# A hybrid decoder layer: the low parts of the input projection's weight tiles made by another engine

## The chip, the cores and the metric

The kernel runs on one core of a Trainium2 chip. The metric is the device time of one execution in microseconds; the median of three runs is compared. The engines are called as in the profile: PE is TensorE (matmul), PEld its weight loads, DVE is VectorE, ACT is ScalarE, POOL is GpSimd, SP is SyncE, which issues the transfers.

## The reference

One layer with a token mixer and a feed-forward part, for a prompt of 1024 positions and 8 x 4 sample positions. The mixer's three groups of heads read one normalised input through one combined input projection:

```python
hn = rms_norm(x, norm_mix_pre[l])
proj = jnp.einsum('bld,de->ble', h, w_in)            # ONE projection for all groups
conv_in, rest = proj[..., :CONV_DIM], proj[..., CONV_DIM:]
conv_out, new_conv = causal_dwconv(conv_in, conv_state, conv_w, conv_b)
conv_out = jax.nn.silu(conv_out)
...                                                   # gated DeltaNet, mLSTM, Mamba-2 SSD, in chunks
mix = jnp.concatenate([o_gdn, h_ml, y_ssd], axis=-1).astype(h.dtype)
out = jnp.einsum('ble,ed->bld', mix, w_out)
```

After it come a residual and a gated feed-forward part with a causal convolution. All inputs and outputs are fp32.

## The kernel before

A product of fp32 matrices is made of three passes in a reduced fp32 format. Each operand is cut into a high part (a cast) and a low part (the operand less its high part), and high x high, high x low and low x high are summed in PSUM (`dense`, lines 275 to 287). The input projection's weights are cut on the chip, tile by tile: `load_w` (lines 263 to 273) takes a tile of 128 x 1024 elements from HBM by a transfer from SP's queue (line 270, three buffers `w`), casts it on ScalarE (line 271, two buffers `wh`), and makes the low part by a subtraction (line 272, two buffers `wl`), on the engine whose operation is given as `tt`; where none is given that is POOL (`gtt`).

The projection has 32 tiles of 128 columns. Two are handled in `begin`, together with the normalisation, and a third is loaded there too (line 642, POOL). The other 29 come from `tile_w` (line 402), called by `gate`, `conv_tile` and `plain_tile`, in the order of the list FILL: the three tiles of each of eight units (four DeltaNet heads, two SSD groups, two mLSTM pairs), and eight gate tiles. Each tile is multiplied with the input in three groups of 352 columns; each group's result stands in one of two PSUM banks (`acc`) until DVE takes it out with a product (`scaled`, line 308). After that a convolved tile has an ACT instruction and three DVE instructions per group (line 473), a tanh on ACT and one more DVE instruction (line 482).

While TensorE works through these tiles, the recurrences of the heads run between them: the DeltaNet's inverse (lines 786 to 871, with line 792 among them), its scan (lines 996 to 1050: 1016 and 1031 on DVE), the SSD batches (lines 1176 to 1238: POOL's lines 1190, 1198 and 1205, DVE's 1189 and 1211), the mLSTM steps. In the first stretch the small rows of gates are made (lines 649 to 737: 703, 712, 720). The order of the work on TensorE is written out by hand, by a planner (`Weave`) that interleaves generators by rank and by times in the table WAIT; the projection has rank 9, the recurrences have ranks 0 to 5. The order on the other engines is made by the tile framework's scheduler from priorities: what has a rank below 8 gets a higher priority than the projection's instructions, its loads included, and otherwise the place in the program counts. Each engine and SP's queue then work through their own list in order. An instruction that has to wait holds what stands behind it.

Of the kernel before, what the change touches and what calls it, by code (L numbers as in the profile page):

```python
# [23 lines left out]
KD = D // P  # L24
# [29 lines left out]
TILE_ORDER = [(s, i) for _, _, ts in UNITS for s, i, _ in ts] + GATES  # L54
# [143 lines left out]
def kernel(ctx: ExitStack, tc: tile.TileContext, I, O):  # L198
# [24 lines left out]
    vtt = nc.vector.tensor_tensor  # L223
# [39 lines left out]
    def load_w(src, kk, w=None, parts=None, cuts=1, tt=gtt):  # L263

        if w is None:
            w = wp.tile([P, kk, P], F32, name="w", bufs=3)
        wh, wl = parts or [wp.tile([P, kk, P], F32R, name=f"w{x}") for x in "hl"]
        for c in range(cuts):
            ks = slice(kk * c // cuts, kk * (c + 1) // cuts)
            dma(out=w[:, ks], in_=src[:, ks])  # L270
            nc.scalar.copy(out=wh[:, ks], in_=w[:, ks])  # L271
            tt(out=wl[:, ks], in0=w[:, ks], in1=wh[:, ks].bitcast(F32), op=ALU.subtract)  # L272
        return wh, wl
# [99 lines left out]
    with ExitStack() as ph:  # L373
# [28 lines left out]
        def tile_w(s, i):  # L402
            if (s, i) in early:
                return early.pop((s, i))
            return load_w(I["w_in"][TILE_ORDER.index((s, i))], KD)

        gated = {}

        def gate(s, i, m):

            w = tile_w(s, i)
            room = cvp.tile([P, 1083], F32, name="pre") if s != "mo" else None
            x = room if s == "gg" else mix[m]
            for g in range(NG):
                a, b = g * G, (g + 1) * G
                ps = yield from dense(accp, w, hn_operand, KD, g)
                scaled(x[:, a:b], ps, g, 0, G)
                if s == "mo":
                    act(out=x[:, a:b], in_=x[:, a:b], func=AF.Tanh, scale=0.5)
                    continue  # L420
                th = room[:, groups[(g + 1) % NG]]
                act(out=th, in_=x[:, a:b], func=AF.Tanh, scale=0.5)

                n = b
                if s == "gg":
                    n = min(max(512 * min(max(done["outs"] - 2 * i, 0), 2), a), b)
                    gated[i] = b
                    if n < b:
                        stt(out=mix[m][:, n:b], in0=th[:, n - a:], scalar=1.0, in1=x[:, n:b], op0=ALU.add, op1=ALU.mult)
                if n > a:  # L430
                    stt(out=x[:, a:n], in0=th[:, :n - a], scalar=1.0, in1=x[:, a:n], op0=ALU.add, op1=ALU.mult)
                    if s == "gg":
                        vtt(out=mix[m][:, a:n], in0=mix[m][:, a:n], in1=x[:, a:n], op=ALU.mult)
# [23 lines left out]
        def conv_tile(s, i, t, y):  # L457
            begun = early_pre.pop((s, i), None)
            pre = conv_in(t) if begun is None else begun
            if begun is None:  # L460
                w = tile_w(s, i)
            blk = samples_of(pre)
            for g in range(NG):
                if begun is None:
                    ps = yield from dense(accp, w, hn_operand, KD, g)
                    conv_scaled(pre, ps, g)
                else:
                    yield lambda: rows_ln
                a, b = g * G, (g + 1) * G if g < 2 else 1080
                act(out=y[:, a:b], in_=pre[:, a + 3:b + 3], func=AF.Identity, bias=cw2[:, 72 + t:73 + t],  # L470
                    scale=cw2[:, 4 * t + 3:4 * t + 4])
                for j in (2, 1, 0):
                    stt(out=y[:, a:b], in0=pre[:, a + j:b + j], scalar=cw2[:, 4 * t + j:4 * t + j + 1], in1=y[:, a:b],
                        op0=ALU.mult, op1=ALU.add)
                if g == 2:
                    gcopy(out=conv_o[:, t, 0:3], in_=pre[:, 1024:1027])
                    gcopy(out=conv_o[:, t, 3:27].rearrange("p (b s) -> p b s", s=3), in_=blk[:, :, 4:7])

                th = act(out=pre[:, a:b], in_=y[:, a:b], func=AF.Tanh)
                if begun is not None:  # L480
                    in_order(th, rows_ln[0])
                stt(out=y[:, a:b], in0=pre[:, a:b], scalar=1.0, in1=y[:, a:b], op0=ALU.add, op1=ALU.mult)

        def plain_tile(s, i, y):
            w = tile_w(s, i)
            for g in range(NG):
                ps = yield from dense(accp, w, hn_operand, KD, g)
                if g < 2:
                    scaled(y[:, g * G:(g + 1) * G], ps, g, 0, G)
                else:  # L490
                    scaled(y[:, 2 * G:SEQ], ps, g, 0, 320)
                    scaled(samp(y), ps, g, 320, 352)
# [1727 lines left out]
```

## Time and profile before

| what | value |
|---|---|
| median of 3 runs | 1541.13 us (1540.32 to 1542.04) |
| the profiled execution's own time | 1540.03 us |
| its span, first to last instruction | 1538.2 us |
| PE busy | 1455.7 us (95%) |
| DVE busy | 1012.1 us (66%) |
| ACT busy | 604.9 us (39%) |
| POOL busy | 610.8 us (40%) |
| line 272 on POOL, tiles `wl`, whole kernel | 42 instructions, 105.2 us |

Busy times are of one profiled execution. An engine's line gives its busy time, its share of the span and its number of instructions. A group's line gives the line of the kernel, engine, operation, output and inputs, shape and count, then its busy time, the mean of one in ns, and the idle time just before its members with what ended it. A timeline's row gives the start and the duration in us, and in brackets the idle time in front of it and what ended that; rows of equal instructions in a row are merged ("x5"), and their duration is then that of all. The ends of matmuls are modelled.

### The profile page before, as it was taken

How to read it: one execution, taken by the hardware profiler on the slowest of the kernel's cores; microseconds unless marked ns; L12 is line 12 of the kernel's file. 1: busy time of each engine (PE TensorE's matmuls, PEld its weight loads, DVE VectorE, ACT ScalarE, POOL GpSimd, SP SyncE). 2: the span in 40 equal slices, each digit the busy share in tenths (PEclk: the TensorE clock that was granted, in tenths of full speed). 3: DMA queues.
4: the chain of work that ended last, by engine and by line, in shares of the span. 5: the costliest groups of instructions: out<-in, count | busy, mean ns of one | idle time of the engine just before them, and what ended most of it. 6: DMA issues, size and time to landing. Idle time of an engine off the chain costs nothing. (4 is left out here: it accounts for less than half of the span.)

```text
span 1538.2 us, 27512 instructions
## 1 busy us (share of the span) xinstructions
PE 1455.7 (95%) x10756; PEld 1410.1 (92%) x10756; DVE 1012.1 (66%) x2013; ACT 604.9 (39%) x1316; POOL 610.8 (40%) x672
## 2 busy tenths in 40 slices
PE   8888999989989989999999999999999999999997
PEld 8787998888989989889889999999999999999996
DVE  6889878697375457723679777766666685334447
ACT  7644544532432333423676433333333344202222
POOL 6234433341343464366641543444344341212234
PEclk9989999999999999999999999999999999999999
DMA  7111010100112032312640222122222136312304
GB/s 225 30 50 31 23 44 27 36 22 28 44 48 69 32 106 85 124 55 91 215 152 34 92 83 73 61 70 84 71 84 83 71 124 219 126 42 98 112 29 156
DMA packets 60362, 124.92 MB, mean 81 GB/s; under 512 B 15544, under 2 KB 21560, under 8 KB 59720
## 3 DMA queue, kind: packets, MB, share of 16 engines
q1 hardware_dynamic: 60232, 123.16, 24.3%
q8 instruction: 85, 1.39, 0.4%
q14 instruction: 45, 0.37, 0.1%
HBM read 97.40 MB, written 25.21 MB: 80 GB/s over the span
## 5 line engine op out<-in xcount | busy, mean ns | idle before, releaser
L208 PE MATMUL acc<-h,wh 128*128 128x264 f32 (+1 forms) x3008 | 672.1, 314 | 17.9 <-DVE pre L308 12.6
L208 PEld LDWEIGHTS acc<-h,wh 128*128 128x128 f32 x3008 | 491.8, 191 | 24.7 <-DVE pre L308 8.9
L208 PE MATMUL acc<-h,wl 128*128 128x264 f32 (+1 forms) x1512 | 462.0, 306 | 0.5 <-POOL wl L619 0.5
L208 PEld LDWEIGHTS acc<-h,wl 128*128 128x128 f32 x1512 | 287.7, 190 | 1.7 <-POOL wl L619 1.6
L208 PE MATMUL acc<-hidl,wh 128*128 128x264 f32 x576 | 163.7, 284 | 0.5 <-DVE hidl L2040 0.5
L208 PE MATMUL acc<-hidh,wh 128*128 128x264 f32 x576 | 163.9, 285 | 0.0
L208 PE MATMUL acc<-hidh,wl 128*128 128x264 f32 x576 | 163.5, 284 | 0.0
L1881 POOL TENSOR_TENSOR wl<-ws,wh 128x512 fp32r<-128x512 f32 x60 | 89.3, 1495 | 159.7 <-ACT wh L1880 155.1
L2063 DVE TENSOR_TENSOR fa<-fa,acc 128x264 f32<-128x264 f32 x160 | 68.3, 428 | 125.4 <-PE acc L208 124.7
L272 POOL TENSOR_TENSOR wl<-w,wh 128x1024 fp32r<-128x1024 f32 x42 | 105.2, 2505 | 68.3 <-ACT wh L271 65.5
L208 PE MATMUL acc<-n,wh 128*128 128x264 f32 x672 | 126.1, 284 | 0.0
L1881 POOL TENSOR_TENSOR wl<-w,wh 128x512 fp32r<-128x512 f32 x40 | 65.3, 1634 | 115.4 <-ACT wh L1880 115.4
L208 PEld LDWEIGHTS acc<-hidl,wh 128*128 128x128 f32 x576 | 108.6, 189 | 0.8 <-DVE hidl L2040 0.8
L208 PEld LDWEIGHTS acc<-hidh,wl 128*128 128x128 f32 x576 | 108.6, 189 | 0.0
L208 PEld LDWEIGHTS acc<-hidh,wh 128*128 128x128 f32 x576 | 108.5, 188 | 0.0
L2054 POOL TENSOR_TENSOR wl<-w,wh 128x1024 fp32r<-128x1024 f32 (+1 forms) x22 | 47.6, 2163 | 148.3 <-ACT wh L2053 145.3
L208 PEld LDWEIGHTS acc<-n,wh 128*128 128x128 f32 x672 | 103.9, 188 | 0.3 <-ACT sq L217 0.3
L208 PE MATMUL acc<-n,wl 128*128 128x264 f32 x336 | 96.1, 286 | 2.8 <-POOL wl L1881 2.8
L208 PE MATMUL acc<-r,wh 128*128 128x264 f32 x480 | 90.9, 286 | 2.8 <-DVE rs L1857 2.7
L208 PEld LDWEIGHTS acc<-r,wh 128*128 128x128 f32 x480 | 74.1, 188 | 4.9 <-DVE rs L1857 4.7
L1813 DVE SCALAR_TENSOR_TENSOR fy<-fpre,vec,fy 128x1072 f32<-128x1072 f32 x44 | 73.7, 1700 | 1.3 <-ACT fy L217 0.8
L2053 ACT CAST wh<-w 128x1024 fp32r<-128x1024 f32 (+1 forms) x22 | 20.5, 933 | 132.3 <-PE acc L208 127.7
(539 smaller groups left out, 3033.1 us busy)
## 6 DMA issues: line engine op xcount, KB each, us to landing
w<-in_w_in_dram SPq DMA_DIRECT2D x30, 512.0 KB
w<-in_w_up_dram SPq DMA_DIRECT2D x60, 256.0 KB
hid_dram<-hid SPq DMA_DIRECT2D x22, 528.0 KB
hidl<-hid_dram SPq DMA_DIRECT2D x21, 528.0 KB
w<-in_w_dn_dram SPq DMA_DIRECT2D x17, 512.0 KB
w<-in_w_out_dram SPq DMA_DIRECT2D x16, 512.0 KB
E<-rows_dram SPq DMA_DIRECT2D x24, 256.0 KB
n<-in_w_up_dram SPq DMA_DIRECT2D x20, 256.0 KB
```

Source lines behind the costliest of these rows:

```text
L208: return nc.tensor.matmul(out, **kw)
L272: tt(out=wl[:, ks], in0=w[:, ks], in1=wh[:, ks].bitcast(F32), op=ALU.subtract)
L1813: stt(out=y[:, :LF], in0=pre[:, j:j + LF], scalar=col(V_FW + 3 * f + j), in1=y[:, :LF], op0=ALU.mult, op1=ALU.add)
L1881: tt(out=wl, in0=x, in1=wh.bitcast(F32), op=ALU.subtract)
L2053: nc.scalar.copy(out=wh, in_=w)
L2054: gtt(out=wl, in0=w, in1=wh.bitcast(F32), op=ALU.subtract)
L2063: vtt(out=fa[:, q, m, :], in0=fa[:, q, m, :], in1=ps[:, :Q], op=ALU.add)
```

## The change

The subtraction of line 272 is issued to DVE (`vtt`) instead of POOL for the tiles that `tile_w` loads, 29 in number. The tile loaded at line 642, the two of `begin` (line 619) and all other users of `load_w` stay as they were.

```diff
         def tile_w(s, i):
             if (s, i) in early:
                 return early.pop((s, i))
-            return load_w(I["w_in"][TILE_ORDER.index((s, i))], KD)
+            return load_w(I["w_in"][TILE_ORDER.index((s, i))], KD, tt=vtt)
```

## Rows read from the trace of the kernel before

**Rows 1.** The page, busy time, share of the span and instructions of each engine.

```profile
PE 1455.7 (95%) x10756; PEld 1410.1 (92%) x10756; DVE 1012.1 (66%) x2013; ACT 604.9 (39%) x1316; POOL 610.8 (40%) x672
```

**Rows 2.** Stretches: length, busy PE, PEld, DVE, ACT, POOL; PE clock, DMA share, GB/s.

```profile
60.00:140.00 80.00, 64.05 (x357) 61.24 (x358) 72.48 (x166) 37.82 (x94) 30.07 (x48) 0.87 0.15 39
60.00:640.00 580.00, 533.37 (x3531) 511.51 (x3532) 416.17 (x1032) 232.72 (x661) 228.83 (x319) 0.97 0.17 49
```

**Rows 3.** Waits of PE, 45 to 640 us: total, times, longest.

```profile
PE acc L208 <- DVE pre L308: 12.6, 5, 4.3
```

**Rows 4.** Groups of POOL, 46 to 630 us.

```profile
L272 POOL TENSOR_TENSOR wl<-w,wh 128x1024 fp32r<-128x1024 f32 x29 | 71.8, 2476 | 44.4 <-ACT wh L271 41.6 <-PE po L208 2.4
```

**Rows 5.** Timelines of POOL and DVE about 106 us, DVE at 99.81.

```profile
106.02 2.40 POOL L272 TENSOR_TENSOR wl<-w,wh 128x1024 fp32r<-128x1024 f32 x1 [5.13 <-ACT wh L271]
...
106.37 2.43 DVE L482 SCALAR_TENSOR_TENSOR kq<-pre,kq 128x352 f32<-128x352 f32 x1 [0.73 <-ACT pre L217]
...
99.81 0.52 DVE L482 SCALAR_TENSOR_TENSOR kq<-pre,kq 128x352 f32<-128x352 f32 x1
```

**Rows 6.** Timeline of DVE beside the first and the last of the 29.

```profile
46.79 3.44 DVE L473 SCALAR_TENSOR_TENSOR kq<-li,cw,kq 128x352 f32<-128x352 f32 x2
...
622.62 2.88 DVE L1066 TENSOR_TENSOR gsq<-hml,gss 128x512 f32<-128x512 f32 x1 [1.75 <-POOL gss L1065]
```

**Rows 7.** Timeline of DVE, two subtractions of SBUF operands after 640 us.

```profile
650.57 1.25 DVE L1583 TENSOR_TENSOR h<-mix,h 128x1056 fp32r<-128x1056 f32 x1
...
738.18 1.59 DVE L272 TENSOR_TENSOR h<-w,h 128x1024 fp32r<-128x1024 f32 x1 [2.75 <-ACT h L271]
```

**Rows 8.** Timelines of DVE and PE, 70 to 79 us.

```profile
70.40 3.24 DVE L712 TENSOR_TENSOR re<-cum,ms 4x1024 f32<-4x1024 f32 x1
...
74.39 1.22 DVE L720 TENSOR_TENSOR seg<-re,few 4x1024 f32<-4x1024 f32 x1
...
78.83 0.59 PE L208 MATMUL acc<-h,wh 128*128 128x352 f32 x2 [3.28 <-DVE pre L308]
```

**Rows 9.** Timelines of DVE (about 93 and 220 us) and PE.

```profile
92.96 3.54 DVE L792 TENSOR_TENSOR two<-NT,con 32x128 f32<-32x128 f32 x4
...
220.34 1.16 DVE L792 TENSOR_TENSOR two<-NT,con 32x128 f32<-32x128 f32 x4
...
98.45 0.96 PE L208 MATMUL acc<-h,wh 128*128 128x352 f32 x2 [3.70 <-DVE pre L308]
```

**Rows 10.** Timelines of DVE and PE, 121 to 130 us.

```profile
121.80 3.84 DVE L792 TENSOR_TENSOR two<-NT,con 32x128 f32<-32x128 f32 x4
...
129.01 0.93 PE L208 MATMUL acc<-h,wh 128*128 128x352 f32 x2 [4.34 <-DVE pre L308]
```

**Rows 11.** Timelines of DVE (about 341 and 76 us) and PE.

```profile
341.08 4.84 DVE L473 SCALAR_TENSOR_TENSOR kq<-pre,cw,kq 128x352 f32<-128x352 f32 x5
...
75.75 2.59 DVE L473 SCALAR_TENSOR_TENSOR v<-pre,cw,v 128x352 f32<-128x352 f32 x5
...
348.68 0.48 PE L212 MATMUL mb<-con,v 128*128 128x128 f32 x1 [4.80 <-DVE vn L990]
```

**Rows 12.** Timelines of POOL and PE, 440 to 448 us.

```profile
440.31 2.40 POOL L272 TENSOR_TENSOR wl<-w,wh 128x1024 fp32r<-128x1024 f32 x1
...
447.96 0.38 PE L208 MATMUL mb<-xw,bn 128*128 128x128 f32 x1 [3.13 <-POOL xw L1198]
```

**Rows 13.** Busy time by stretch, two stretches behind stalls, columns as in rows 2.

```profile
97.00:103.80 6.80, 5.35 (x18) 5.35 (x19) 6.54 (x20) 2.38 (x4) 0.63 (x3) 0.50 0.26 78
...
448.60:452.00 3.40, 3.03 (x12) 3.03 (x13) 3.36 (x9) 0.32 (x1) 1.12 (x4) 0.50 0.01 2
```

**Rows 14.** Busy time by stretch, one POOL instruction of line 272, columns as in rows 2.

```profile
404.13:406.52 2.39, 2.39 (x19) 2.39 (x18) 0.44 (x2) 0.33 (x1) 2.39 (x3) 1.00 0.00 0
```

**Rows 15.** Groups of ACT, 46 to 630 us.

```profile
L271 ACT CAST wh<-w 128x1024 fp32r<-128x1024 f32 x29 | 30.3, 1047 | 18.4 <-PE acc L208 16.3 <-PE mc L208 1.1 <-DMA inv<-X 1.0
```

**Rows 16.** Waits of SP's queue, 40 to 640 us: total, times, longest.

```profile
SPq L270 <- POOL wl L272: 198.9, 25, 15.1
```

## The prediction

> **What bounds the kernel now.** Start with the page: TensorE is busy for 95% of the span [rows 1]. So only time in which TensorE stands still, or runs at its lower clock, can be won or lost. The change touches instructions between 46 and 630 us. The table of stretches for 60 to 640 us [rows 2] leaves TensorE 580.0 - 533.4 = 46.6 us without work at a mean granted clock of 0.97, and its first 80 us are the worst: DVE is busy for 72.5 of 80 us there and the clock is 0.87. The view of waits [rows 3] then names the largest group: TensorE waits 12.6 us in five places for DVE's eviction of a projection bank (line 308). In this stage DVE decides how long TensorE stands still, and the change gives DVE more work. By that alone it should lose time. The timeline says why it is not that simple.
>
> **The lock between POOL and DVE.** One weight tile's low part costs POOL about 2.4 us, 29 times, 71.8 us in all [rows 4]. Look at what DVE does meanwhile. At 106.02 POOL begins one of 2.40 us; at 106.37 DVE begins line 482, and ends 2.43 us later, at 108.80, 0.4 us after POOL; the same line takes 0.52 us at 99.81 [rows 5]. A DVE instruction with both inputs in SBUF that meets this POOL instruction is held until POOL has ended. For all 29 I took the DVE instructions that overlap POOL's, and from each one's time the shortest time of its line and shape (for line 712, which has no second, that of line 720): 20 of the 29 hold DVE by more than 0.4 us, and the sum is 34.6 us. The first and the last of the 29 are line 473 (two instructions, 3.44 us, at 46.79) and line 1066 (2.88 us, at 622.62) [rows 6].
>
> **The change, part by part.** (a) Removed: 29 POOL instructions, 71.8 us [rows 4]. POOL does not bound, so this is worth something only where POOL's queue is late, below. (b) Added: 29 DVE instructions of 128x1024. No trace shows exactly this one without POOL beside it; the nearest row is line 1583, also a subtraction of two SBUF operands, 1.25 us for 1056 columns, so 1.21 us for 1024. The dearest is line 272 itself, which one output-projection tile already gives to DVE: 1.59 us, with POOL at the same work next to it [rows 7]. So 29 x 1.21 = 35.1 us, at most 29 x 1.59 = 46.1 us; I take 1.21, because the POOL instruction that made 1.59 of it is the one that goes. (c) DVE gets back the 34.6 us. DVE's bill is thus nearly even, +0.5 us (up to +11.5), and what counts is where it is paid.
>
> Four large stalls stand directly behind a lock (I count the 29 tiles from 1). Tile 2: line 712 takes 3.24 us where the same shape takes 1.22 (line 720), 2.0 lost; TensorE then stands 3.28 us at 78.83 [rows 8]. Tile 3: four of line 792 take 3.54 us instead of 1.16, 2.4 lost; TensorE stands 3.70 us at 98.45 [rows 9]. Tile 5: the same four take 3.84 us; TensorE stands 4.34 us at 129.01 [rows 10]. Tile 14: five of line 473 take 4.84 us instead of 2.59, 2.25 lost; TensorE stands 4.80 us at 348.68 [rows 11]. If DVE's own instruction lies ahead of what TensorE waits for, each gains the loss less 1.21: 0.8 + 1.2 + 1.1 + 1.0 = 4.1 us (for tile 5 about what tile 3 has). If it lies behind, the whole loss comes back, 9.0 us. The trace of before cannot say, since DVE's order is new; I take the first.
>
> A fifth stall is POOL's own: at 440.31 its 2.40 us stand ahead of the products of the SSD step, and TensorE waits 3.13 us for the last of these at 447.96 [rows 12]. Of 2.40 I take 2.0, as a DVE instruction feeds that product too. The clock adds to it: behind the stall of tile 3, TensorE had a granted 0.50, that is 1.2 instead of 2.4 GHz, from 97.0 to 103.8, and behind this fifth one from 448.6 to 452.0 [rows 13]. A stall of about 1 us should leave the clock alone, as the smaller ones of this stage did, so half of 3.4 us, 1.7, is won at the fifth. The stalls of the four others would still be 2.3 to 3.8 us, so there I count no clock.
>
> What it adds: in nine of the 29 tiles DVE loses next to nothing to POOL now. In six of these DVE is idle for 1.7 to 2.0 us inside POOL's 2.4, as at 404.13, where it works for 0.44 of 2.39 us [rows 14]; 1.21 us is free there, and it is not free if DVE has caught up with work by then. The other three cost 3 x 1.21 = 3.6 us of DVE and between 0 and 3.6 of TensorE; I take 1, because the two banks between TensorE and DVE let an eviction be late.
>
> The wait that is added: DVE's instruction waits for ScalarE's cast (line 271), 1.05 us, and the cast in turn for TensorE to let go of the buffer; ScalarE is idle for 16.3 us in front of the 29 casts for that reason alone [rows 15]. While DVE waits, the evictions and the scan steps behind it in its queue wait too, and TensorE for them. POOL could bear that. But the eviction of the tile that let go of the buffer is ready sooner and takes part of that time. I cost it at nothing beyond the 1 us, and at its full price in a rival. The low part itself is early: with two buffers it is made while TensorE works through the tile before, and no wait of TensorE in a projection bank names line 272, so neither 1.2 us sooner nor some later is seen. Loads: SP's queue stands 198.9 us in 25 places at line 270 until POOL has read the tile of three loads before [rows 16]. It will now stand until DVE has. DVE is 1.2 us quicker, but may begin later; the small transfers of the inverse queued behind move with it. The weights themselves are asked for three tiles ahead: nothing either way.
>
> One rule speaks against the change. The Trainium skill, Perfetto Trace Analysis, section Optimizing Scalar/DVE Operations, says that POOL and DVE share a read port of SBUF, so that moving work between these two may not help, and that work should leave DVE when DVE is saturated. That the port is shared this trace shows (the held line 482, [rows 5]); by the rule the sum would be zero, my second rival. By the rows, the side that holds the lock holds it half as long.
>
> **Sum.** 4.1 + 2.0 + 1.7 - 1.0 = 6.8 us less. The profiled execution took 1540.03 us, its span 1538.2 with 1.8 around it; the median of the runs is 1.1 above it. So 1531.4 for the span, 1533.2 for such an execution, 1534.3 for the median. With 1.59 us for each instruction the four stalls give 1.5 less and the three tiles 0.3 more: 1536.
>
> **Rivals.** Full relief: DVE's instruction, which stands late in the order of the program, lies behind what TensorE waits for. Then 9.0 + 2.4 us, the clock behind the fifth stall, 1.7, and that behind the four others: after tile 3's stall it was low from 98.45 to 103.8, half of which is 2.7 us; four times that is 10.7, and I take 9. Together about 22: 1519 us. For it: DVE is full around those stalls. Against: all four would have to fall right.
> No change: what DVE gets back it pays elsewhere, 35.1 against 34.6, and POOL's gain ends in a wait for DVE: 1541, give or take 3. For it: the even bill, and the rule above.
> Slower: DVE reaches its new instruction early, and stands at the head of its queue until the cast has ended. Full price: 1.05 us of waiting and 1.21 of work, 29 x 2.26 = 65.5 us, less the 34.6 and less about 11 us of idle time in the six tiles: 20 us more on DVE. The locks' 34.6 us now stand before stalls of 3.28 + 3.70 + 4.34 + 4.80 = 16.1, so half passes on: +10, less the fifth stall's 3.7, +6: 1547 us. For it: casts start just when TensorE lets go, and the scans of the DeltaNet wait on single DVE steps. It decides from about 0.6 us of waiting per tile: 29 x 0.6 = 18 us, which with the 35.1 eats up the 34.6, the idle 11 and, at half, POOL's 3.7 (worth 7.4 on DVE).
>
> **Chances.** My forecast, 1534 (1529 to 1538), 0.42; full relief 0.10; no change 0.22; slower 0.26. About 0.2% (3 us) is what a measurement of this kernel can tell from no change, so faster 0.52, within it 0.22, slower 0.26. The range from 1522 to 1549 leaves out most of the full relief and the far end of the slower case, where the price per tile is 1.59 us.
>
> **What would show it.** Right: line 272 on DVE at 1.2 to 1.4 us, 29 times; lines 792, 473, 482 and 712 without members of over 2 us near it; TensorE's wait for line 308 below 9 us; the stall near 448 down to about 1 us with a full clock. Wrong: DVE idle in front of line 272 by more than 0.5 us on average, with new stalls of TensorE for lines 308, 1016 or 1031 behind it; or the same total of TensorE's idle time at other places, which would be the even bill. If other engines' orders change as well, stalls could appear in places that no row here points to, and that would make it wrong without any of these steps.

## The result and the profile after

| | before | after |
|---|---|---|
| median of 5 runs each, same chip | 1541.08 us (1535.37 to 1542.04) | 1521.04 us (1520.30 to 1522.34) |
| ratio | | 0.9888 (95%: 0.9871 to 0.9905) |
| the profiled execution's own time, its span | 1540.03, 1538.2 | 1520.56, 1518.7 |

The kernel became 20.0 us (1.1%) faster. The forecast was 1534.3 us with a range from 1522 to 1549: the sign was right, the gain three times too small, and the time lies 1 us below the range.

First the engines, from the page of after (as [rows 1]):

```profile
PE 1445.3 (95%) x10756; PEld 1401.9 (92%) x10756; DVE 1002.1 (66%) x2042; ACT 604.0 (40%) x1316; POOL 547.2 (36%) x643
```

DVE has 29 instructions more and is busy for 10.0 us less in the whole kernel, 5.1 of them in weight tiles 1 to 29 and 4.5 behind the output projection, where both kernels do the same. The new instruction and its waits stand in the groups of DVE, 46 to 630 us (line, engine, operation, shapes, count, then busy time, mean ns of one, idle time before it):

```profile
L272 DVE TENSOR_TENSOR wl<-w,wh 128x1024 fp32r<-128x1024 f32 x29 | 35.7, 1233 | 4.6 <-ACT wh L271 4.5
...
L473 DVE SCALAR_TENSOR_TENSOR kq<-pre,cw,kq 128x376 f32<-128x376 f32 x24 | 17.5, 728 | 1.8 <-ACT kq L217 1.6
...
L792 DVE TENSOR_TENSOR two<-NT,con 32x128 f32<-32x128 f32 x32 | 11.5, 359 | 0.4
...
L482 DVE SCALAR_TENSOR_TENSOR v<-pre,v 128x352 f32<-128x352 f32 x10 | 5.4, 538 | 1.9 <-ACT pre L217 1.8
```

The same three lines in the kernel before, the same view:

```profile
L473 DVE SCALAR_TENSOR_TENSOR kq<-pre,cw,kq 128x376 f32<-128x376 f32 x24 | 22.9, 954 | 1.6 <-ACT kq L217 1.5
L792 DVE TENSOR_TENSOR two<-NT,con 32x128 f32<-32x128 f32 x32 | 17.2, 538 | 0.3
...
L482 DVE SCALAR_TENSOR_TENSOR v<-pre,v 128x352 f32<-128x352 f32 x10 | 9.0, 895 | 2.7 <-ACT pre L217 2.4
```

A subtraction costs DVE 1.233 us, and the wait for the cast is 4.5 us for all 29, 0.16 us each. Lines that were held take less, though POOL's other instructions still hold some: line 473 has one member of 2.62 us at 427.93, beside POOL's line 1190. By the reckoning of [rows 5] and [rows 6], for 45 to 640 us, POOL's line 272 held DVE for 35.7 us before (30 instructions, one of them of the output projection) and for 4.1 us after (three of the output projection, which comes earlier). Over weight tiles 1 to 29 alone, all of POOL's instructions together held DVE for 53.8 us before and 20.0 us after, so 33.8 us went. (Here a hold is what a DVE instruction beside one of POOL's takes beyond the shortest of its kind in any run, counted from 0.1 us.)

The stretches (columns as in [rows 2]):

```profile
60.00:140.00 80.00, 68.34 (x414) 65.65 (x414) 72.65 (x182) 37.27 (x96) 23.75 (x50) 0.91 0.14 39
60.00:640.00 580.00, 541.46 (x3630) 520.17 (x3631) 426.26 (x1094) 243.44 (x685) 176.94 (x298) 0.98 0.18 52
```

The 580 us now hold 541.5 us of TensorE's work instead of 533.4, and 3630 of its groups instead of 3531. But TensorE's largest waits, 45 to 640 us, changed less than this leads one to expect:

```profile
PE acc L208 <- DVE pre L308: 11.9, 5, 5.3
PE mb L212 <- DVE vn L990: 3.8, 4, 2.8
...
PE mb L208 <- POOL xw L1198: 2.6, 3, 1.6
```

The first one was 12.6 us in [rows 3]. So the gain did not come from the row on which the forecast began.

Since both kernels give TensorE the same 10756 instructions in the same order, its time can be compared between the same instructions. I cut it at its instructions 250, 700, 3740 and 5400: from 250 to 700 are weight tiles 1 to 5, to 3740 tiles 6 to 29, to 5400 the output projection and the start of the feed-forward part. "Gaps" is TensorE's idle time, "low clock" the time with a granted clock of 0.50:

| stretch | before: us, gaps, low clock | after: us, gaps, low clock |
|---|---|---|
| I, tiles 1 to 5 | 96.7, 18.1, 20.5 | 89.3, 14.6, 13.7 |
| II, tiles 6 to 29 | 479.8, 30.7, 17.1 | 467.1, 23.3, 6.8 |
| III, output projection | 235.9, 11.2, 13.7 | 236.6, 13.3, 6.8 |
| IV, the rest, to TensorE's last instruction | 667.0 | 667.4 |

I and II give 20.1 us. Gaps are 3.5 + 7.4 = 10.9 of them. The other 9.2 are TensorE's own time on the same instructions. The time at low clock is 17.1 us shorter; at 1.2 instead of 2.4 GHz half of such a time is lost where TensorE works, so at most 8.5 us of the 9.2. This is one pair of executions: the other four of the kernel after had a mean granted clock of 0.982 to 0.985 against 0.989 here, and yet ended between 0.2 us earlier and 1.9 us later.

The single stalls (TensorE, same instruction before and after):

| stall | before | after | forecast of the gain |
|---|---|---|---|
| tile 2 [rows 8] | 3.28 | 1.53 at 74.40 | 0.8 |
| tile 3 [rows 9] | 3.70 | 5.26 at 94.01 | 1.2 |
| tile 5 [rows 10] | 4.34 | 3.82 at 122.13 | 1.1 |
| tile 14 [rows 11] | 4.80 | 2.78 at 335.31 | 1.0 |
| POOL's own [rows 12] | 3.13 | 1.59 at 431.52 | 2.0 |
| tile 10, not in the forecast | 2.96 | 0.31 at 247.19 | 0 |

Tile 10 in the timelines of before (PE, POOL, DVE; start, us, engine, line, then in brackets the idle time before and what ended it):

```profile
254.04 0.65 PE L212 MATMUL mb<-con,H 128*128 128x128 f32 x2 [2.96 <-DVE E L914]
...
248.36 2.39 POOL L272 TENSOR_TENSOR wl<-w,wh 128x1024 fp32r<-128x1024 f32 x1
...
250.71 1.08 POOL L965 TENSOR_TENSOR kw<-kw,sm 128x512 f32<-128x512 f32 x1
...
250.06 1.87 DVE L792 TENSOR_TENSOR two<-NT,con 32x128 f32<-32x128 f32 x2
```

and the same place after, DVE and PE:

```profile
242.47 1.22 DVE L272 TENSOR_TENSOR wl<-w,wh 128x1024 fp32r<-128x1024 f32 x1
...
245.81 0.86 DVE L792 TENSOR_TENSOR two<-NT,con 32x128 f32<-32x128 f32 x3
...
247.19 0.44 PE L212 MATMUL mb<-con,H 128*128 128x128 f32 x2 [0.31 <-DVE vn L990]
```

Before, POOL's subtraction ends at 250.75, and two of line 792, 0.58 us together elsewhere, take until 251.93. The hold is only about 1.3 us, smaller than those I had picked, but it stands in front of a DVE step that feeds TensorE. The subtraction itself holds the first of the two for some 0.6 us; the second begins at 250.90 and is held by line 965, which stood behind the subtraction in POOL's queue. So here the queue has a part: in pool_fill below, where POOL works as long without reading, this stall is 1.28 us, in after 0.31. After, DVE makes the subtraction ahead of line 914's instructions, and three of line 792 take 0.86 us.

Tile 3 shows the opposite. DVE, then PE, after:

```profile
89.10 1.16 DVE L792 TENSOR_TENSOR two<-NT,con 32x128 f32<-32x128 f32 x4
...
91.39 1.22 DVE L272 TENSOR_TENSOR wl<-w,wh 128x1024 fp32r<-128x1024 f32 x1
...
93.44 0.94 DVE L308 TENSOR_TENSOR pre<-acc,rs 128x352 f32<-128x352 f32 x2
...
94.01 0.96 PE L208 MATMUL acc<-h,wh 128*128 128x352 f32 x2 [5.26 <-DVE pre L308]
```

The four of line 792 take 1.16 us instead of 3.54, yet the stall grew by 1.6 us: TensorE had come sooner, and the 1.22 us and two of line 482 stand ahead of the eviction.

The clock behind stalls (columns as in [rows 2], the third number from the end is the granted clock). Before, behind the stalls of tiles 10 and 14:

```profile
254.10:257.50 3.40, 3.40 (x16) 3.33 (x17) 1.95 (x6) 0.37 (x1) 0.00 (x0) 0.50 0.03 2
346.20:353.00 6.80, 4.32 (x17) 4.33 (x18) 5.47 (x16) 2.21 (x5) 0.36 (x2) 0.50 0.15 55
```

After, behind the stall of tile 14, behind the fifth, and behind that of tile 3:

```profile
335.30:342.00 6.70, 6.47 (x47) 6.29 (x47) 6.58 (x22) 0.59 (x2) 0.00 (x0) 1.00 0.01 4
...
432.50:435.90 3.40, 3.37 (x14) 3.37 (x15) 3.36 (x10) 0.28 (x1) 1.12 (x4) 0.50 0.00 0
...
91.10:97.90 6.80, 3.89 (x13) 3.89 (x14) 6.40 (x13) 1.69 (x3) 1.91 (x6) 0.50 0.30 86
```

The two stalls themselves, after:

```profile
335.31 0.44 PE L212 MATMUL mb<-con,v 128*128 128x128 f32 x2 [2.78 <-DVE vn L990]
...
431.52 0.49 PE L208 MATMUL mb<-xw,bn 128*128 128x128 f32 x2 [1.59 <-POOL xw L1198]
```

Behind 2.78 us the clock stayed whole, behind 1.59 us it fell. The forecast had it the other way round for both.

### The profile page after: what moved, and what is told of

It reads as the page before. It is cut to its first block, busy times and chain, and to the rows that moved or that the text cites. A ratio compares the mean times of both kernels' runs of the same rounds, so it can differ in the third digit from the quotient of the medians.

```text
span 1518.7 us, 27495 instructions
## 1 busy us (share of the span) xinstructions
PE 1445.3 (95%) x10756; PEld 1401.9 (92%) x10756; DVE 1002.1 (66%) x2042; ACT 604.0 (40%) x1316; POOL 547.2 (36%) x643
## 5 line engine op out<-in xcount | busy, mean ns | idle before, releaser
L208 PE MATMUL acc<-h,wh 128*128 128x264 f32 (+1 forms) x3008 | 669.4, 313 | 16.6 <-DVE pre L308 11.9
L208 PEld LDWEIGHTS acc<-h,wh 128*128 128x128 f32 x3008 | 489.2, 190 | 23.3 <-DVE pre L308 13.5
L2053 ACT CAST wh<-w 128x1024 fp32r<-128x1024 f32 (+1 forms) x22 | 20.5, 933 | 132.4 <-PE acc L208 127.7
L1880 ACT CAST wh<-ws 128x512 fp32r<-128x512 f32 x60 | 36.1, 618 | 91.0 <-PE acc L208 88.1
```

The costliest lines, as they stand in the source:

```text
L208: return nc.tensor.matmul(out, **kw)
L1880: nc.scalar.copy(out=wh, in_=x)
L2053: nc.scalar.copy(out=wh, in_=w)
```

## The experiments

Theory: POOL's subtraction reads SBUF and holds DVE's instructions with two SBUF inputs; the gain is the end of these holds, less what DVE's own 35.7 us cost TensorE. Rivals: the gain is the room in POOL's queue; or the new order of the instructions (a comparison of the two traces takes out and puts in 331 rows of DVE's order, 82 of ACT's, 83 of POOL's and 18 of SP's, the 29 subtractions counted in); and, of what DVE pays, that its place in the queue does harm. Ratios are to the kernel before, run beside each on the same chip; its medians there were 1534.4 to 1536.9 us.

**pool_read.** The kernel after, and POOL works again for each tile: two subtractions that read the high part and whose result nobody uses. The orders of DVE, ACT and SP are those of after, row for row.

```diff
+        scr = nat.tile([P, KH, P], F32, name="scr")
...
-            return load_w(I["w_in"][TILE_ORDER.index((s, i))], KD, tt=vtt)
+            wh, wl = load_w(I["w_in"][TILE_ORDER.index((s, i))], KD, tt=vtt)
+            for a in (0, KH):
+                gtt(out=scr, in0=wh[:, a:a + KH].bitcast(F32), in1=wh[:, a:a + KH].bitcast(F32), op=ALU.subtract)
+            return wh, wl
```

> The changed kernel, and for each of the 29 tiles two subtractions of 128x512 on POOL more, which read the high part in SBUF and write a scratch tile that nobody reads; they start when the cast has ended, as line 272 did on POOL. The orders of DVE, ACT and SP are those of the changed kernel, word for word. Theory 1 (the lock: DVE is held while POOL reads SBUF): about 32 us of holding come back on DVE, and the 20 us with them: 1535 to 1545 us. Theory 2 (POOL's queue: what stands behind line 272 on POOL came earlier): the same, 1535 to 1545. Theory 3 (the scheduler's new order of DVE and ACT happens to be better): order unchanged, so 1521 to 1525.

**pool_fill.** The same, but POOL's work for each tile only writes: five fills of 128x512. A one-column copy of ACT ties them to the cast. But for these copies, ACT's order is that of after with one instruction moved, and DVE's with six rows exchanged near 573 us.

```diff
...
+            nc.scalar.copy(out=scr[:, 0, 0:1], in_=wh[:, 0, 0:1].bitcast(F32))
+            for n in range(5):
+                nc.gpsimd.memset(scr, 0.0)
```

> The changed kernel, and for each of the 29 tiles five memsets of 128x512 on POOL more, about 2.4 us together, tied to the cast by a copy of one column on ACT (0.2 us); POOL is as busy as with line 272, but these read nothing from SBUF. Theory 1 (the lock): nothing holds DVE, 1521 to 1526 us. Theory 2 (POOL's queue): 1535 to 1545. Theory 3 (order): 1521 to 1525.

Measured: pool_read 1546.38 us, 1 us above the range expected, ratio 1.0059 (1.0039 to 1.0079); pool_fill 1522.64 us, 0.9896 (0.9867 to 0.9924). The groups of POOL, 46 to 640 us, first of pool_read:

```profile
L408 POOL TENSOR_TENSOR scr<-wh 128x512 f32<-128x512 f32 x58 | 80.7, 1392 | 48.3 <-ACT wh L271 46.1
```

then of pool_fill:

```profile
L409 POOL MEMSET scr<- 128x512 f32 x145 | 76.2, 526 | 43.5 <-ACT scr L407 37.3
```

POOL is busy for nearly as long in both (before: 71.8 us, [rows 4]), but one loses the whole gain and the other nothing. DVE in pool_read, at tile 2:

```profile
69.23 1.89 DVE L272 TENSOR_TENSOR wl<-w,wh 128x1024 fp32r<-128x1024 f32 x1
71.15 1.22 DVE L716 TENSOR_TENSOR re<-cum,ms 4x1024 f32<-4x1024 f32 x1
...
73.12 1.95 DVE L724 TENSOR_TENSOR seg<-re,few 4x1024 f32<-4x1024 f32 x1
```

which meet these two of POOL:

```profile
67.85 2.19 POOL L408 TENSOR_TENSOR scr<-wh 128x512 f32<-128x512 f32 x1 [0.88 <-ACT wh L271]
...
72.65 1.33 POOL L408 TENSOR_TENSOR scr<-wh 128x512 f32<-128x512 f32 x1
```

and in after, the same rows of DVE (lines 712 and 720 there):

```profile
67.75 1.23 DVE L272 TENSOR_TENSOR wl<-w,wh 128x1024 fp32r<-128x1024 f32 x1
69.01 1.22 DVE L712 TENSOR_TENSOR re<-cum,ms 4x1024 f32<-4x1024 f32 x1
...
70.98 1.22 DVE L720 TENSOR_TENSOR seg<-re,few 4x1024 f32<-4x1024 f32 x1
```

By the same reckoning POOL's new work holds DVE for 27.2 us in pool_read and for 3.1 us in pool_fill; all of POOL's instructions over tiles 1 to 29 hold it for 44.6 and 20.5 us. The stretches of the table: I 96.6 and II 487.2 us in pool_read, 89.3 and 470.3 in pool_fill. TensorE's largest wait, 45 to 640 us, in pool_read:

```profile
PE acc L208 <- DVE pre L308: 17.5, 5, 6.4
```

and in pool_fill:

```profile
PE acc L208 <- DVE pre L308: 11.4, 5, 5.3
```

So it is the holding, and hardly the room in POOL's queue or the order: after's order with holds is slower than the kernel before. The Trainium skill states this rule (SBUF — State Buffer, section Who interferes with whom): a DVE instruction with two SBUF inputs contends with a GpSimd instruction that reads SBUF, and not with one that only writes. The two runs agree. The pair also gives the price of a hold, since DVE's own work is the same in both: 24.1 us of holds more cost 23.7 us of time (24.2 us in stretches I and II), about 1 us for each.

**none.** The low parts of the 29 tiles are not made at all: the third product takes the high part instead, so the result lacks that term. TensorE's work is unchanged.

```diff
-        wh, wl = parts or [wp.tile([P, kk, P], F32R, name=f"w{x}") for x in "hl"]
+        if low_part:
+            wh, wl = parts or [wp.tile([P, kk, P], F32R, name=f"w{x}") for x in "hl"]
+        else:
+            wh = wp.tile([P, kk, P], F32R, name="wh")
+            wl = wh
...
-            return load_w(I["w_in"][TILE_ORDER.index((s, i))], KD, tt=vtt)
+            return load_w(I["w_in"][TILE_ORDER.index((s, i))], KD, low_part=False)
```

> The changed kernel without any low part for the 29 tiles (the third product takes the high part a second time, so TensorE does the same work and the output lacks that term). DVE has neither the lock nor the price of 29 x 1.23 = 35.7 us. If the price is free, because DVE's instruction lies in gaps, 1519 to 1523 us; if half of DVE's time passes on to TensorE, as my slower rival had it, about 1521 - 18 = 1503.

**double.** The kernel after with two more subtractions of 128x512 on DVE for each tile, result unused.

```diff
...
+            for a in (0, KH):
+                vtt(out=scr, in0=wh[:, a:a + KH].bitcast(F32), in1=wh[:, a:a + KH].bitcast(F32), op=ALU.subtract)
```

> The changed kernel, and for each of the 29 tiles two subtractions of 128x512 on DVE more (about 1.4 us together, 40 us in all) into a scratch tile. If DVE's time is free in this stage, 1521 to 1526 us; if half passes on, about 1541; if what counts is the time by which DVE is held at the few places before the large stalls, 1525 to 1535.

Measured: none 1504.5 us (0.9787, 0.9753 to 0.9822), double 1528.62 us (0.9943, 0.9920 to 0.9966). Against after, 1521.04, the 35.7 us of DVE cost 16.5 us (15.6 by the ratios); the next some 40 us cost 7.6 (8.5). So between a fifth and a half of DVE's price passes on. The share isn't one number: DVE's order differs from after's in none and in double, and I have no run that keeps it. With holds gone and no price, the change would have brought 33 (by the ratio) to 37 us; it brought 20.

**first5** and **rest24.** Only tiles 1 to 5 are given to DVE, or only tiles 6 to 29.

```diff
+        taken = [0]
...
+            taken[0] += 1
-            return load_w(I["w_in"][TILE_ORDER.index((s, i))], KD, tt=vtt)
+            return load_w(I["w_in"][TILE_ORDER.index((s, i))], KD, tt=vtt if taken[0] <= 5 else gtt)
```

> Only tiles 1 to 5 (46 to 145 us) have their low part made by DVE, the other 24 by POOL as before. My forecast put 3.1 of its 6.8 us here (stalls at 78.83, 98.45 and 129.01): 1538 us against a before of 1541. By full relief the three stalls give 6.7 us and some 6 us of clock: 1528. By the traces of before and after, in which TensorE is 7.4 us ahead at the end of this stretch: 1533.

> Only tiles 6 to 29 (145 to 630 us) have their low part made by DVE, the first five by POOL as before. My forecast put 3.7 us here (stalls at 348.68 and 447.96): 1537. If the two parts add up as in the traces of before and after (20.6 - 7.4 = 13.2 us), 1528.

Measured: first5 1535.38 us (0.9999, 0.9984 to 1.0013), rest24 1520.76 us (0.9897, 0.9870 to 0.9923). So first5 gained nothing where 3 to 13 us were expected, and rest24 13.7 us by the medians, 15.8 by the ratio, near the 13 that the traces of before and after gave. The whole gain is that of tiles 6 to 29, although three of the four large stalls of the forecast belong to tiles 2, 3 and 5. In first5's trace stretch I is as short as in after, 89.3 us, but stretch II takes 484.0 instead of 479.8 us. There DVE's order differs from that of before until 173.9 us, beside tile 7; behind that only the times at which things meet have moved. Three stalls (PE) are new or longer: the first two are not in before and stand where the order still differs, the third is 1.18 us in before:

```profile
148.25 0.49 PE L208 MATMUL mc<-S,kq 128*128 128x128 f32 x2 [1.57 <-DVE S L1031]
...
173.50 0.49 PE L208 MATMUL mc<-r,Gt 128*128 128x128 f32 x2 [2.00 <-DVE r L1018]
...
589.05 0.49 PE L208 MATMUL mb<-va,kwm 128*128 128x130 f32 x2 [2.59 <-DVE kwm L1122]
```

Stretch II is longer by 4.2 us than in before, which takes back part of what five tiles won; whether by the new order or by the new meetings with POOL's 24 tiles, no run tells. The rest of the missing gain is open: the profiled execution of before is a long one (1540 us; beside first5 the median of before was 1534.4), so the 7.4 us of stretch I may be large by chance.

**urgent.** The 29 subtractions at the priority of the recurrences, so that DVE takes them as early as it can.

```diff
+        def urgent(**kw):
+            with tc.high_priority(offset=FIRST):
+                return vtt(**kw)
...
-            return load_w(I["w_in"][TILE_ORDER.index((s, i))], KD, tt=vtt)
+            return load_w(I["w_in"][TILE_ORDER.index((s, i))], KD, tt=urgent)
```

> The changed kernel with the 29 subtractions at the priority of the recurrences' work, so that they come earlier in DVE's list; DVE should then meet more of them before the cast has ended, which is the slower rival's mechanism (in the changed kernel it stands 4.5 us there in all). If waiting at the head of DVE's queue costs TensorE time, 1523 to 1530 us, with DVE's idle time in front of line 272 well above 4.5 us; if it is nothing beside the lock, 1519 to 1523.

Measured: 1518.2 us (0.9881, 0.9858 to 0.9903). DVE, 46 to 640 us:

```profile
L401 DVE TENSOR_TENSOR wl<-w,wh 128x1024 fp32r<-128x1024 f32 x29 | 36.0, 1241 | 3.4 <-ACT wh L271 3.3
```

By its ratio it is not told apart from after. The priority did little: in DVE's order it moved nine of the 29 ahead, by one to eight places, and left the others. They wait for the cast for only 3.3 us in all. The slower rival needed 0.6 us per tile; it is off by a factor of five here, but a DVE that comes early at every tile was not made.

**split4.** The kernel before, POOL's subtraction cut into four of 128x256: if the length of one hold counts, this should win.

```diff
...
-            tt(out=wl[:, ks], in0=w[:, ks], in1=wh[:, ks].bitcast(F32), op=ALU.subtract)
+            for i in range(n):
+                a, b = kk * i // n, kk * (i + 1) // n
+                tt(out=wl[:, a:b], in0=w[:, a:b], in1=wh[:, a:b].bitcast(F32), op=ALU.subtract)
...
-            return load_w(I["w_in"][TILE_ORDER.index((s, i))], KD)
+            return load_w(I["w_in"][TILE_ORDER.index((s, i))], KD, n=4)
```

> The kernel before, with each of the 29 subtractions on POOL cut into four of 128x256 (about 0.65 us each by the rows of other sizes, so POOL works a little longer in all). If DVE is held for as long as one POOL instruction reads, DVE can slip in between two of them and is held at most about 0.7 us instead of 2.4: the sum of holding falls well below 30 us, and the time to 1524 to 1533 us. If POOL keeps DVE out until its whole work on a tile is done, or if what costs is POOL's share of the time and not the length of one hold, no change from the kernel before.

Measured: 1535.09 us (0.9993, 0.9977 to 1.0010), no change. Timelines of POOL and DVE about 119 us:

```profile
119.37 3.63 POOL L274 TENSOR_TENSOR wl<-w,wh 128x256 fp32r<-128x256 f32 x4
...
119.47 3.92 DVE L475 SCALAR_TENSOR_TENSOR v<-pre,cw,v 128x352 f32<-128x352 f32 x4
```

and the group of POOL, 46 to 630 us:

```profile
L274 POOL TENSOR_TENSOR wl<-w,wh 128x256 fp32r<-128x256 f32 x116 | 96.8, 862 | 43.8 <-ACT wh L271 40.9 <-PE po L208 2.4
```

The two engines now take turns: four short DVE instructions (about 0.6 us each alone) stretch over 3.92 us. POOL's total rises from 71.8 to 96.8 us and the holding falls only from 35.7 to 26.3 us. Shorter pieces are no cure; less reading by POOL is.

**more.** The default engine of `load_w` becomes DVE. That moves 13 more low parts: the tile of line 642, eight of the output projection and four of line 1682. That is fewer than the 16 that were expected: seven of line 1653 name POOL themselves and stay there.

```diff
-    def load_w(src, kk, w=None, parts=None, cuts=1, tt=gtt):
+    def load_w(src, kk, w=None, parts=None, cuts=1, tt=vtt):
```

> The changed kernel with every other low part of load_w on DVE too: the tile loaded before the 29, eleven tiles of the output projection, four of the up projection (16 instructions). If the lock is what costs and DVE has room there (57% busy between 700 and 800 us), 1513 to 1519 us; if POOL's part of that stretch holds nothing TensorE waits for, 1521.

Measured: 1511.05 us (0.9836, 0.9814 to 0.9857), 10 us less than after, below the 1513 to 1519 expected, and all of it in stretch III: 226.2 instead of 236.6 us, gaps 6.8 instead of 13.3. (In the runs that leave this stretch as it is, it took 233.0 to 236.4 us.) Waits of PE there, after (625 to 870 us):

```profile
PE po L208 <- POOL fpre L1806: 3.0, 1, 3.0
PE acc L208 <- DVE h L1583: 2.9, 2, 2.4
...
PE acc L208 <- POOL fpre L1806: 1.6, 1, 1.6
PE acc L208 <- DVE ss L1634: 1.5, 1, 1.5
```

and in more (615 to 860 us):

```profile
PE acc L208 <- DVE h L1583: 1.6, 1, 1.6
...
PE acc L208 <- POOL fpre L1806: 0.7, 1, 0.7
PE acc L208 <- DVE ss L1634: 0.6, 1, 0.6
```

Here POOL's own queue is late too (line 1806), so this gain is not of holds alone.

**more_urgent**, **more_masks**, **more_begin.** Three additions to more: urgent's priority; the 24 mask additions of 128x512 of lines 876 and 954 on DVE, and three smaller ones behind them; the 12 subtractions of line 619 on DVE.

```diff
-            gtt(out=E, in0=E, in1=bc(con[:, mask:mask + P], 1, n), op=ALU.add)
+            vtt(out=E, in0=E, in1=bc(con[:, mask:mask + P], 1, n), op=ALU.add)
...
-                gtt(out=E, in0=E, in1=bc(con[:, C_NEG:C_NEG + P], 1, 4), op=ALU.add)
+                vtt(out=E, in0=E, in1=bc(con[:, C_NEG:C_NEG + P], 1, 4), op=ALU.add)
```

> All of load_w's low parts on DVE, and the 29 at the priority of the recurrences. If the gains of the two (10 us and 3 us by the runs so far) add up, 1507 to 1510 us; if the 3 us were an order that came out well by chance, 1510 to 1513.

> All of load_w's low parts on DVE, and the 24 additions of masks of 128x512 (1.3 us each on POOL) as well. In the changed kernel these hold DVE for some 9.6 us in all, and would cost it 24 x 0.69 = 16.6 us. If a hold costs more than as much work of DVE's own, 1505 to 1511 us; if DVE's bill decides, 1511 to 1518.

> All of load_w's low parts on DVE, and the twelve of 128x256 in the first 45 us as well, where DVE is busy for 70% of the time. TensorE waits for POOL there for less than 1 us in all. If DVE has room, 1509 to 1511 us; if the evictions and the splitting of the input on DVE come later, 1512 to 1518.

Measured: more_urgent 1512.69 us (0.9839, 0.9811 to 0.9868), so urgent's 3 us do not add, if they are any; more_masks 1501.98 us (0.9770, 0.9742 to 0.9798); more_begin 1508.85 us (0.9822, 0.9793 to 0.9851), not told apart from more. more_masks lies below the 1505 to 1518 expected and beats both kernels, the one before by 2.3% (1535.61 beside it, 34 us) and after by 19 us. Its masks on DVE, 46 to 640 us:

```profile
L876 DVE TENSOR_TENSOR E<-E,con 128x512 f32<-128x512 f32 x16 | 12.7, 791 | 12.2 <-DMA E<-rows_dram 7.9 <-ACT eg L217 4.3
...
L954 DVE TENSOR_TENSOR E<-E,con 128x512 f32<-128x512 f32 x8 | 5.4, 677 | 0.0
```

On POOL they took 20.7 and 11.6 us and held DVE for some 11 us; on DVE they cost it 18.1, that is 7 more, and the kernel is still 9 us faster than more. Either a hold costs TensorE more than the same time of DVE's own work, as pool_read and pool_fill beside double say, or the masks, now 0.7 to 0.8 us instead of 1.3 to 1.4, were late themselves. No run tells these apart for the masks.

## Why the forecast was right in sign and too small

Right:
- *The lock.* That POOL's reading holds DVE, and that this is what the change can remove, is shown by pool_read against pool_fill. POOL's 71.8 us of busy time as such were worth little in the projection's stage (pool_fill's 76.2 us cost 1.6 us, within its interval).
- *The even bill.* 29 x 1.21 = 35.1 against 34.6 us; measured 35.7 against 33.8.
- *The wait for the cast, costed at nothing.* 0.16 us per tile. The slower rival falls with it for this order of DVE.
- *The fifth stall.* Forecast down by 2.0, measured by 1.54 us.
- *The place in DVE's queue.* I took the new instruction to lie ahead of what TensorE waits for. It does: at tile 2 (67.75 against the eviction at 73.83) and at tile 3 (91.39 against 93.44).
- *The signs.* Of lines 792, 473, 482 and 712 one member over 2 us is left (2.62 us), and the stall near 448 fell to 1.59 us, but without the full clock behind it.
- *Loads.* SP's waits at line 270 for the low part fell from 198.9 us in 25 places [rows 16] to 69.7 in 10 on DVE and 18.9 in 2 on POOL, and no wait of TensorE shows it.

Wrong:
- *The four large stalls as the whole of the effect.* They gave 3.28 + 3.70 + 4.34 + 4.80 = 16.12 less 1.53 + 5.26 + 3.82 + 2.78 = 13.39, that is 2.7 us, where I had 4.1, and the full relief 9.0. (By its rows tile 5 lost 3.84 less 1.16, 2.7 us, and not the 2.3 that its 1.1 stands for.) All gaps of I and II gave 10.9 where I had 4.1 + 2.0 - 1.0 = 5.1. The step that failed is the choice of only the stalls directly behind a hold of 2 us or more: 20 tiles held DVE by over 0.4 us, and what they cost stood in stalls I had not listed (tile 10: 2.65 us; 279.56 in before, 1.37 us, gone in after). I let holds count at four places and charged DVE's new 1.21 us there in full; the runs show that a hold passes on about whole (24.1 us of holds, 23.7 us of time) and DVE's own work by a fifth to a half. By that, 33.8 us of holds less a fifth to a half of 35.7 us make 16 to 27 us; measured are 20. rest24 shows it on the chip: I gave tiles 6 to 29 1.0 + 2.0 + 1.7 - 1.0 = 3.7 us, they are worth 1.03% of 1534, 15.8 us (interval 11.8 to 20; 13.7 by the medians).
- *"There I count no clock."* The term was 1.7 us; by the stretches at 0.50 it is up to 8.5 in the profiled pair. What failed is the assumption that a stall of 2.3 to 3.8 us keeps the clock low behind it as before and one of about 1 us does not. After, 2.78 us left it at 1.00, 1.59 us did not.
- *"TensorE's wait for line 308 below 9 us"* as the sign of being right: it is 11.9. The gain did not go through that row.
- *Full relief at 1519 with a chance of 0.10.* The number came, the mechanism did not: it needed all four stalls to fall, and one grew.
- *The rule I weighed.* The Trainium skill, Perfetto Trace Analysis, section Optimizing Scalar/DVE Operations, says that moving work between these two engines might not help. Here it did, by 20 us, and by 34 with more of it. The even bill was there, as the rival said; but a microsecond in which DVE is held cost more than one in which it works in its own order.

That last sentence rests on whole runs and sums (pool_read against pool_fill, double against after; 35.7 us of work for 33.8 us of holds, 20 us won) and is not shown by one row; in double, unlike the first pair, DVE's order changed as well. A likely reason, argued and not shown, is place: the order of DVE's own instruction is fixed, and a hold falls on whatever meets POOL.

## What to carry to other kernels

When one engine's instructions hold another's, do not charge a moved instruction by its time on either engine: sum the holds over every instruction that meets it, and then give the whole sum a share that passes on (here 0.2 to 0.5 for DVE's own time, about 1 for holds), not only the few stalls that stand right behind. To find out whether an engine's queue or its reading does the harm, give it work of the same length that reads nothing. And price the clock with the stalls: in the profiled pair TensorE's own time fell by 9.2 us beside 10.9 us of gaps. One pair alone does not settle that share.

## What the runs showed of the hardware that was not expected

- Cutting POOL's instruction into four made it 35% dearer in total (96.8 against 71.8 us) beside a busy DVE and left the time where it was.
- The length of a stall did not decide the granted clock behind it: 1.00 behind 2.78 us, 0.50 behind 1.59 us in one and the same execution.
- A microsecond by which DVE was held cost about a microsecond of the kernel (24.1 us of holds, 23.7 us of time, pool_read against pool_fill), where a microsecond of DVE's own added work cost 0.2 (39.7 us, 7.6 us of time, double against after).
- Whether kernels with holds vary more is open. Beside first5, before ran between 1531.2 and 1541.0 us (13 runs), and rest24 only between 1519.5 and 1522.0 (4); but none, where POOL makes no low part of these tiles, ran between 1502.9 and 1511.2 (4).
